# Later column sums and earlier value transposes at the layer boundary of a two-layer hybrid decoder step on one Trainium2 core

## The chip, the cores and the metric

The kernel runs on one core of one Trainium2 chip. The metric is device time in microseconds: before, the median of three runs is 1918.96 us (1916.27, 1918.96 and 1923.78). Lower is better.

## What is computed

One inference step of a decoder with two layers, for 1024 prompt tokens and 8 sample tokens that share the weights. Each layer normalises its input with a root mean square over the 1024 channels, projects it, runs several branches (layer 0: gated delta rule, dilated attention, attention to a memory; layer 1: a gated recurrence and the memory attention), projects back, normalises again and adds the residual. Each layer also projects 256 memory tokens to the keys and values of its memory attention. The part that matters here, from the reference:

```python
def rms_norm(x, g):
    xf = x.astype(F32)
    y = xf * lax.rsqrt(jnp.mean(xf * xf, axis=-1, keepdims=True) + EPS)
    return (y * g.astype(F32)).astype(x.dtype)

def memory_kv(mem, g, w_kv):
    B, M, _ = mem.shape
    return (rms_norm(mem, g) @ w_kv).reshape(B, M, 2, MEM_HEADS, MEM_HD)

    for layer in range(DEPTH):
        mkv_p = memory_kv(mem_prompt, mem_norm[layer], w_mem_kv[layer])
        hp = rms_norm(xp, norm_pre[layer])
        ...
        xp = xp + rms_norm(mix_p.astype(xp.dtype) @ w_out, norm_post[layer])
```

## The kernel before

Channels lie on the 128 partitions (8 tiles of 128 channels), tokens along the free axis. The 1032 tokens are cut into three chunks `CH` of 352, 336 and 344, called 0, 1 and 2. Every large product is made three times in reduced precision (`mm3`, L164 to L166): high part of the weights by high part of the input, high by low, low by high. So each weight tile is loaded, cast to its high part by ScalarE (L152) and subtracted to its low part by GpSimd or VectorE (L154), with three buffers each for the loaded, high and low tiles; the inputs are split in the same way (L228, L229).

The change lies at the boundary of the two layers, in `out_layer` of layer 0. Its second half runs the last output projection over chunk 2 (`one`, products `wo00p2` to `wo07p2`), while chunks 0 and 1 are normalised beside it by generators, `chain(0)` and `chain(1)`; behind it `chain(2)` starts, and `mem_kv(1, ...)` makes the keys (`mk10` to `mk13`) and values (`mv10` to `mv13`) of layer 1 from the 256 memory tokens. Then layer 1 (`odd`) begins with its first products: `wq10` and `wx0` over chunks 0 and 1, then over chunk 2, and `wx1`. The chunk-2 products wait for chunk 2's normalised input `h1..2.`.

A `chain(ci)` makes, for its chunk: the column sums of the post-norm (`po..c`, L199), a reciprocal square root in 12 small VectorE operations on 128x3 elements (L200, L115 to L120) and a diagonal of it (`po..d`, L205); a product with a tile of ones that spreads it over the partitions (`po..b`, L208); the scaling of `y` (L1463) and the residual add (L1464, odd channel tiles on VectorE, even ones on GpSimd). Then the pre-norm of layer 1 in `chan_rstd`: squares on ScalarE (L215), added in pairs on VectorE (L217), column sums `pr.c`, small operations, diagonal `pr.d`, `pr.b`, and `norm_split` (L226 to L229), which writes `h1`.

Each `yield n` in a generator hands control back until the n-th following `tick()`. Every projection ticks once for each chunk it finishes. What a generator issues at a tick is held behind the last instruction that each engine was given at that time; beyond that the scheduler sets the order of each engine's queue. TensorE takes its queue strictly in order: an instruction that waits holds all behind it.

In `mem_kv` each value tile is projected to `vf` with channels on partitions and copied out of PSUM (L323), then turned by two TensorE transposes into a PSUM tile `mvt` (L346) and copied to `vt` by VectorE (L347). For layer 1 this turning is a generator on a lane `turn`; one PSUM buffer (pool `a`, one buffer in this stretch) serves all four.

Of the kernel before, what the change touches and what calls it, by code (L numbers as in the profile page):

```python
# [65 lines left out]
def body(ctx, tc, I, O):  # L66
# [56 lines left out]
    for g in range(3):  # L123
        n = (LEN[g] - 1) * 1024
# [62 lines left out]
            except StopIteration as e:  # L187
                return e.value

    def tok_rstd(pool, sqs, n, scale, name, pt=None):  # L190

        nb = -(-n // P)
        pt = pt or ctile
        cols = pt(f"{name}c")
        x, y, t = (pool.tile([P, nb], F32, name=f"{name}{i}", tag=f"tr{i}{nb}", bufs=2) for i in "xyt")
        for b in range(nb):
            o = min(b * P, n - P)
            for k, sq in enumerate(sqs):
                T.matmul(cols[:, b:b + 1], sq[:, o:o + P], ones[:, 0:1], start=k == 0, stop=k == len(sqs) - 1)  # L199
        V.tensor_scalar(x, cols[:, :nb], scale, EPS, op0=ALU.mult, op1=ALU.add)  # L200
        rsqrt(y, x, t)
        dg = pool.tile([P, CW], F32, name=f"{name}d", tag="dg", bufs=1)
        for b in range(nb):
            o, w = b * P, min(P, n - b * P)
            V.tensor_scalar(dg[:, o:o + w], ident[:, P - w:], y[:, b:b + 1], None, op0=ALU.mult)  # L205
        yield 1
        bc = pt(f"{name}b")
        T.matmul(bc[:, :n], ones, dg[:, :n], start=True, stop=True)  # L208
        return bc[:, :n]

    def chan_rstd(pool, xc, n, name):
        sqs = []
        for k in range(8):
            sq = pool.tile([P, CW], F32, name=f"{name}sq{k}", tag=f"sq{k % 2}", bufs=1 if k % 2 else 4)
            S.activation(sq[:, :n], xc[k], AF.Square)  # L215
            if k % 2:
                V.tensor_tensor(sqs[-1][:, :n], sqs[-1][:, :n], sq[:, :n], ALU.add)  # L217
            else:
                sqs.append(sq)
        yield 1  # L220
        return (yield from tok_rstd(pool, sqs, n, 1.0 / 1024.0, name))

    def norm_split(pool, xc, n, gname, gi, rs, outs, name, hb=2):
        for k in range(8):
# [10 lines left out]
    def start(lane, gen, lag=0):  # L235

        lanes.setdefault(lane, []).append([gen, lag])
# [80 lines left out]
    def mem_kv(l, mem, pool, part=None):  # L318
        outs, rs = mem

        def put(dst, ps):
            if rs is None:
                S.copy(dst, ps)  # L323
            else:
                V.tensor_tensor(dst, ps, rs, ALU.mult)
        if part != 1:
            kts[l] = cst.tile([P, 4, 256], F32, name=f"kt{l}", tag="kt", bufs=1)
            vts[l] = cst.tile([P, 2, 4, P], F32, name=f"vt{l}", tag="vt", bufs=1)
        kt, vt = kts[l], vts[l]
        for h in range(4 if part != 1 else 0):  # L330
            def dk(ci, c0, n, ps, h=h):
                put(kt[:, h, :], ps)
            proj([I["wmem"][l, h]], outs, f"mk{l}{h}", dk, chunks=(0,))
        if part != 1:
            nc.scalar.dma_start(out=O["memk"][l], in_=kt)
        for h in range(4 if part != 0 else 0):
            vf = pool.tile([P, 256], F32, name=f"vf{l}{h}", tag="vf", bufs=2)

            def dv(ci, c0, n, ps, vf=vf):
                put(vf, ps)  # L340
            proj([I["wmem"][l, 4 + h]], outs, f"mv{l}{h}", dv, chunks=(0,))
            nc.scalar.dma_start(out=O["memv"][l, :, h, :], in_=vf)
            def turn(h=h, vf=vf):
                pt = ptile(f"mvt{l}{h}")
                for b in range(2):
                    T.transpose(pt[:, b * P:(b + 1) * P], vf[:, b * P:(b + 1) * P], ident)  # L346
                V.tensor_copy(vt[:, :, h, :], pt[:, :256].rearrange("p (b d) -> p b d", b=2))  # L347
                return
                yield
            if l:  # L350
                start("turn", turn())
            else:
                at_once(turn())

    def silu_drain(pool, dst, dst_s, name):
        def f(ci, c0, n, ps):
# [1028 lines left out]
    def out_layer(l, xa, xa_stack, order, late, w0):  # L1385

        with ExitStack() as so:
# [69 lines left out]
            def chain(ci, xr):  # L1457
                c0, n = CH[ci]
# [5 lines left out]
                    (V if k % 2 else G).tensor_tensor(yk[k], yk[k], xr[k], ALU.add)  # L1464
                if l == 0:
                    nc.scalar.dma_start(out=x1d[:, :, c0:c0 + n], in_=t[:, :, :n])
                    rs = yield from chan_rstd(np_, yk, n, f"pr{ci}")
                    if ci == 2:
                        sx.close()
                        h1.extend(new_h(pool(nst, "h1c", "right"), 1, (2,)))  # L1470
                    norm_split(np_, yk, n, "npre", 1, rs, h1[ci], f"hn{ci}", 2)
                else:
                    for i in range(0, 8, 2):
                        nc.sync.dma_start(out=O["yT"][:, i:i + 2, c0:c0 + n], in_=t[:, i:i + 2, :n])
# [10 lines left out]
            if l == 0:  # L1485
                start("norm2", chain(2, xr[2]))
                tick()
                mem_kv(1, mem_reload(pb), np_)
                drain_lanes("turn")
                drain_lanes("norm2")  # L1490
            else:
                with tc.high_priority(offset=HP):
                    at_once(chain(2, xr[2]))
                sx.close()
# [158 lines left out]
```

## Time and profile before

| | |
|---|---|
| median of three runs | 1918.96 us |
| the profiled execution, whole | 1920.67 us |
| its span in the trace | 1918.9 us |
| TensorE matmuls, busy | 1782.3 us (93%) |
| VectorE, busy | 1088.6 us (57%) |
| ScalarE, busy | 715.0 us (37%) |
| GpSimd, busy | 550.6 us (29%) |
| granted TensorE clock, mean | 0.954 of 2.4 GHz |

Times in the views are microseconds from the span's start. PE is TensorE, DVE is VectorE, ACT is ScalarE, POOL is GpSimd. The trace drops the numbers in tile names (`mk10p0` reads `mk10p`). A row of the timeline gives start, duration, engine, line, operation, output and inputs, shape and count; in brackets stands how long the engine sat idle before it, and what ended that wait.

### The profile page before, as it was taken

What the parts mean: (1) busy time and instruction counts of PE and PEld (TensorE: products, weight loads), DVE (VectorE), ACT (ScalarE), POOL (GpSimd) and SP (SyncE); (2) the same over time, 40 slices, a digit from 0 to 9 for tenths busy, and PEclk for the clock granted to TensorE, in tenths of its full rate; (3) what the DMA queues carried; (4) which work ended last, traced back from release to release, by engine and by line L of the source; (5) the groups of instructions that cost most, each with busy time, mean ns of one, the idle gap of its engine ahead of it and who ended that gap; (6) DMA issues with size and microseconds to landing.
All of it is one profiled execution on the core that took longest, in us unless ns stands there. A gap on an engine that the chain in (4) does not pass through costs nothing.

```text
span 1918.9 us, 29175 instructions
## 1 busy us (share of the span) xinstructions
PE 1782.3 (93%) x11341; PEld 1724.7 (90%) x11341; DVE 1088.6 (57%) x2302; ACT 715.0 (37%) x1610; POOL 550.6 (29%) x367
## 2 busy tenths in 40 slices
PE   7999998798999899999999988998499999989996
PEld 6799998698999899999999977998499999988995
DVE  6878759534543314525336376578735647667536
ACT  5355533122322244333333342344223434526432
POOL 3422224222121113231533403215431534331201
PEclk9999998899999899999999998997699999999998
DMA  8435455543344435545644535465633433223554
GB/s 290 180 132 194 181 165 191 193 135 109 114 179 167 177 137 183 205 149 188 213 168 171 169 118 150 131 202 183 234 108 135 143 133 105 84 67 122 152 186 139
DMA packets 160698, 306.25 MB, mean 160 GB/s; under 512 B 25072, under 2 KB 120496, under 8 KB 158640
## 3 DMA queue, kind: packets, MB, share of 16 engines
q1 hardware_dynamic: 67024, 222.47, 33.7%
q10 hardware_dynamic: 93536, 81.93, 13.2%
q8 instruction: 89, 1.46, 0.3%
q14 instruction: 49, 0.40, 0.1%
HBM read 254.05 MB, written 138.28 MB: 204 GB/s over the span
## 4 chain that ended last, share of the span: by engine, by line
PE 73%; DVE 14%; DMA 3%; ACT 3%; issue 2%; ACTq 1%; SPq 0%; POOL 0%; DVEq 0%; POOLq 0%
PE ss L1016 2%; DVE tm L758 1%; PE so L1049 1%; PE mo L401 1%; PE ms L375 1%; PE gz L881 1%; PE gt L886 1%; PE st L1039 1%; DVE xi L760 1%; DVE y L1463 1%; DMA mg<-mixd 1%; DMA mf<-mixd 1%; PE mt L394 1%; DMA gst<-state_gdn 1%; PE svp L1001 1%
## 5 line engine op out<-in xcount | busy, mean ns | idle before, releaser
L1018 DVE CUSTOM_DVE_ANT_0 spr<-ss,cs 128x128 f32<-128x128 f32 (+1 forms) x96 | 32.4, 350 | 90.7 <-PE ss L1016 90.3
L652 DVE SCALAR_TENSOR_TENSOR acc<-pre,vec,acc 128x1024 f32<-128x1024 f32 x36 | 49.2, 1366 | 13.4 <-ACT acc L650 13.2
L1025 ACT ACTIVATE spr<-spr,snm 128x128 f32<-128x128 f32 (+1 forms) x96 | 42.2, 441 | 36.4 <-DVE snm L1020 36.4
L1464 POOL TENSOR_TENSOR y<-y,xr 128x352 f32<-128x352 f32 (+2 forms) x24 | 23.0, 961 | 106.3 <-DVE y L1463 105.8
L381 ACT ACTIVATE pm<-ms,nm 128x256 f32<-128x256 f32 x64 | 29.7, 473 | 49.1 <-DVE nm L379 42.8
L1424 POOL COPY mg<-mixs 128x8 f32<-128x8 f32 x24 | 9.2, 383 | 131.3 <-DVE wo01al L154 48.6
L1409 DVE TENSOR_TENSOR ya<-ya,ysq 128x352 f32<-128x352 f32 (+2 forms) x42 | 26.2, 625 | 32.7 <-ACT ysq L1408 32.5
L1016 PE MATMUL ss<-sw,sw 128*128 128x128 f32 (+1 forms) x192 | 42.4, 322 | 0.0
L1259 DVE TENSOR_SCALAR lacc<-lpre,vec 128x1024 f32<-128x1024 f32 x8 | 19.3, 2418 | 34.0 <-ACT lpre L1249 34.0
L1049 PE MATMUL so<-spt,svt 128*128 128x128 f32 x280 | 38.2, 275 | 0.0
L401 PE MATMUL mo<-mpt,vt 128*128 128x512 f32 x64 | 34.6, 627 | 3.4 <-DVE mpt L396 3.4
L1049 PEld LDWEIGHTS so<-spt,svt 128*128 128x128 f32 x280 | 36.2, 191 | 0.0
L1427 DVE TENSOR_TENSOR mbl<-mg,mbh 128x344 fp32r<-128x344 f32 x24 | 17.2, 715 | 33.3 <-ACT mbh L1426 33.3
L375 PE MATMUL ms<-kt,qm 128*128 128x256 f32 x128 | 33.4, 390 | 0.0
L1262 DVE SCALAR_TENSOR_TENSOR lacc<-lpre,vec,lacc 128x1024 f32<-128x1024 f32 x24 | 32.7, 1363 | 0.3
L375 PEld LDWEIGHTS ms<-kt,qm 128*128 128x128 f32 x128 | 24.6, 198 | 8.9 <-issue 4.9
L1002 DVE COPY svt<-svp 128x512 f32<-128x512 f32 x24 | 15.5, 685 | 28.9 <-PE svp L1001 24.4
L1016 PEld LDWEIGHTS ss<-sw,sw 128*128 128x128 f32 x192 | 31.2, 189 | 0.6 <-DVE sml L1018 0.2
L758 DVE TENSOR_TENSOR tm<-bl,xi 128x1 f32<-128x1 f32 (+30 forms) x31 | 30.3, 976 | 2.5 <-DMA bl<-aqd 2.0
L1272 POOL TENSOR_TENSOR lxl<-lacc,lxh 128x1032 fp32r<-128x1032 f32 x8 | 22.4, 2800 | 30.6 <-ACT lxh L1271 30.6
L1426 ACT CAST mbh<-mg 128x344 fp32r<-128x344 f32 x24 | 11.5, 481 | 52.4 <-DMA mg<-mixd 42.7
L1308 POOL COPY lhl<-lacc 128x1 f32<-128x1 f32 x8 | 4.5, 559 | 89.7 <-DVE lacc L1307 89.7
(2144 smaller groups left out, 7344.8 us busy)
## 6 DMA issues: line engine op xcount, KB each, us to landing
o_sw3s<-cache_swa SPq DMA_DIRECT2D x64, 1023.5 KB
o_sw2s<-cache_swa SPq DMA_DIRECT2D x16, 1022.0 KB
gaq<-aqd ACTq DMA_DIRECT2D x20, 512.0 KB
mf<-mixd SPq DMA_DIRECT2D x19, 344.0 KB
sfb<-fd SPq DMA_DIRECT2D x12, 512.0 KB
aqd<-aq ACTq DMA_DIRECT2D x4, 1024.0 KB
o_sw3p<-sw SPq DMA_DIRECT2D x8, 512.0 KB
mixd<-lgt ACTq DMA_DIRECT2D x8, 512.0 KB
```

The costliest lines, as they stand in the source:

```text
L375: T.matmul(ps[:, b * 256:(b + 1) * 256], q[:, (b0 + b) * P:(b0 + b + 1) * P], kt[:, h, :], start=True, stop=True)
L381: S.activation(pr[:, b2 * 2 + b, :], ps[:, b * 256:(b + 1) * 256], AF.Exp, bias=nm[:, b0 + b:b0 + b + 1], scale=SC, accum_out=lt[:, b0 + b ...
L401: T.matmul(po, vt[:, kb, h, :], sts[kb], start=kb == 0, stop=kb == 1)
L652: V.scalar_tensor_tensor(acc, pre[:, j:j + 1024], vc("gconv", ti * 4 + j), acc, ALU.mult, ALU.add)
L758: V.tensor_tensor(t3, bl[:, 0:i, i][:, None, :].broadcast_to([P, i, i]), xi[:, 0:i, 0:i].rearrange("p j c -> p c j"), ALU.mult)
L1016: T.matmul(po, q[:, bb * P:(bb + 1) * P], k[:, k0:k0 + w], start=True, stop=True)
L1018: V.tensor_tensor_reduce(pr[:, bb, :w], po, mask, 1.0, NEG, ALU.add, ALU.max, accum_out=ml[:, 0, g, bb:bb + 1])
L1025: S.activation(pr[:, bb, :w], pr[:, bb, :w], AF.Exp, bias=nm[:, bb:bb + 1], scale=SC, accum_out=ml[:, 1, g, bb:bb + 1])
L1049: T.matmul(po[:, (bb % 4) * P:(bb % 4 + 1) * P], vt[:, kb, :], pt[:, o:o + P], start=st, stop=sp_)
L1262: V.scalar_tensor_tensor(acc[:, :1024], pre[:, j:j + 1024], vc("lconv", ti * 4 + j), acc[:, :1024], ALU.mult, ALU.add)
L1409: V.tensor_tensor(acc[:, :n], acc[:, :n], sq[:, :n], ALU.add)
L1464: (V if k % 2 else G).tensor_tensor(yk[k], yk[k], xr[k], ALU.add)
```

## The change

The sums of a chunk's pre-norm are asked for two projections behind its squares instead of one (four for chunk 2), and chunk 2's spread product two behind its sums instead of one. The transposes of layer 1's value tiles are issued directly behind their projection, as layer 0's are, instead of at the next tick.

```diff
-    def tok_rstd(pool, sqs, n, scale, name, pt=None):
+    def tok_rstd(pool, sqs, n, scale, name, pt=None, lag=1):
...
-        yield 1
+        yield lag
         bc = pt(f"{name}b")
...
-    def chan_rstd(pool, xc, n, name):
+    def chan_rstd(pool, xc, n, name, lags=(1, 1)):
...
-        yield 1
-        return (yield from tok_rstd(pool, sqs, n, 1.0 / 1024.0, name))
+        yield lags[0]
+        return (yield from tok_rstd(pool, sqs, n, 1.0 / 1024.0, name, lag=lags[1]))
...
-            if l:
-                start("turn", turn())
-            else:
-                at_once(turn())
+            at_once(turn())
...
-                    rs = yield from chan_rstd(np_, yk, n, f"pr{ci}")
+                    rs = yield from chan_rstd(np_, yk, n, f"pr{ci}", ((2, 1), (2, 1), (4, 2))[ci])
...
                 mem_kv(1, mem_reload(pb), np_)
-                drain_lanes("turn")
                 drain_lanes("norm2")
```

No instruction is added or taken away; the scheduler puts them in another order from `wo05p2` up to the first chunk-2 products of layer 1. Before and behind that each engine's order is the same row for row. Lines behind L346 carry a number lower by three in the changed kernel, and those behind L1486 by four.

TensorE's queue from the end of the value projections on (`mv13`), before: the twelve column sums of chunk 2 (`pr2c`), its spread product, then transposes `mvt11` and `mvt12` in and ahead of layer 1's first product `wq10p0`.

```order
L166 MATMUL mv13p0_13011<-mrh13_12634,mv13l0_13007 128x256
L199 MATMUL pr2c_12743<-cs_72,pr2sq0_12691 128x1
L199 MATMUL pr2c_12743<-cs_72,pr2sq2_12696 128x1
...
L199 MATMUL pr2c_12743<-cs_72,pr2sq6_12706 128x1
L208 MATMUL pr2b_12807<-pr2d_12771,cs_72 128x344
L346 MATMUL mvt11_12999<-cs_72,vf11_12928 128x128 x2
L164 MATMUL wq10p0_13106<-h1h00_11834,wq10h0_13100 128x352
...
L346 MATMUL mvt12_13037<-cs_72,vf12_12966 128x128 x2
L164 MATMUL wq10p0_13106<-h1h06_11846,wq10h0_13100 128x352
```

The same place in the changed kernel; `mvt10` and `mvt11` stand further ahead there, inside `mv12` and `mv13`:

```order
L166 MATMUL mv13p0_13015<-mrh13_12634,mv13l0_13011 128x256
L346 MATMUL mvt12_13004<-cs_72,vf12_12916 128x128 x2
L164 MATMUL wq10p0_13106<-h1h00_11834,wq10h0_13100 128x352
...
L199 MATMUL pr2c_12841<-cs_72,pr2sq0_12691 128x1
L166 MATMUL wq10p1_13132<-h1h15_11860,wq10l0_13101 128x336
...
L199 MATMUL pr2c_12841<-cs_72,pr2sq6_12706 128x1
L165 MATMUL wx0p0_13167<-h1l04_11843,wx0h0_13161 128x352
...
L208 MATMUL pr2b_12949<-pr2d_12869,cs_72 128x344
L164 MATMUL wx0p1_13193<-h1h17_11864,wx0h0_13161 128x336
...
L164 MATMUL wq10p2_13219<-h1h20_12955,wq10h0_13100 128x344
```

The 96 rows of `wq10` and `wx0` over chunks 0 and 1 stood behind `pr2b`; now the sums stand among them, behind the 41st to the 61st, and 93 of them are ahead of `pr2b`.

VectorE's queue at the first turned value tile, before: the copy (L347) stands behind the last split of chunk 2 (`h1l27`), in layer 1's set-up work.

```order
L1246 MEMSET lpre1_13287 128x3
L229 TENSOR_TENSOR h1l27_12828<-hn2hf7_12857,h1h27_12827 128x344
L347 COPY vt1_12639<-mvt10_12961 128x2x128
L1219 TENSOR_SCALAR t8_13069<-e8_13068 128x8
L1227 TENSOR_SCALAR n8_13067<-vec_73 128x8
```

In the changed kernel:

```order
L120 SCALAR_TENSOR_TENSOR po02y_12581<-po02t_12582,po02y_12581 128x3
L347 COPY vt1_12639<-mvt10_12874 128x2x128
L205 TENSOR_SCALAR po02d_12598<-cs_72,po02y_12581 128x128 x2
L205 TENSOR_SCALAR po02d_12598<-cs_72,po02y_12581 128x88
L229 TENSOR_TENSOR h1l13_11857<-hn1hf3_12453,h1h13_11856 128x336
```

The copy of `mvt10` now stands in chunk 2's post-norm, ahead of the diagonal `po02d`; before, it stood behind all of chunk 2's pre-norm.

TensorE's queue at the end of the output projection (`wo07p2`), before: chunk 1's sums stand on both sides of the first key projection, and its spread product `pr1b` in the middle of the third.

```order
L166 MATMUL wo07p2_12538<-mbh07_11825,wo07bl1_12534 128x344
L164 MATMUL mk10p0_12646<-mrh00_12604,mk10h0_12641 128x256
...
L199 MATMUL pr1c_12293<-cs_72,pr1sq0_12186 128x1
...
L166 MATMUL mk10p0_12646<-mrh13_12634,mk10l0_12642 128x256
L199 MATMUL pr1c_12293<-cs_72,pr1sq2_12191 128x1
...
L166 MATMUL mk12p0_12781<-mrh10_12622,mk12l0_12777 128x256
L208 MATMUL pr1b_12378<-pr1d_12321,cs_72 128x336
L199 MATMUL po02c_12579<-cs_72,ya02_11933 128x1 x3
```

In the changed kernel:

```order
L166 MATMUL wo07p2_12538<-mbh07_11825,wo07bl1_12534 128x344
L208 MATMUL pr0b_12312<-pr0d_12255,cs_72 128x352
L199 MATMUL pr1c_12346<-cs_72,pr1sq0_12154 128x1
...
L199 MATMUL pr1c_12346<-cs_72,pr1sq6_12169 128x1
L164 MATMUL mk10p0_12646<-mrh00_12604,mk10h0_12641 128x256
...
L166 MATMUL mv10p0_12815<-mrh12_12630,mv10l0_12811 128x256
L208 MATMUL pr1b_12439<-pr1d_12374,cs_72 128x336
L199 MATMUL po02c_12579<-cs_72,ya02_11933 128x1 x3
L164 MATMUL mv10p0_12815<-mrh13_12634,mv10h0_12810 128x256
```

Chunk 0's spread product `pr0b` stood inside `wo07p2` and now stands directly behind it; all of chunk 1's sums follow it; `pr1b` and the post-norm sums of chunk 2 (`po02c`) have moved behind 54 more rows, into the fifth of the eight projections.

## Rows read from the trace of the kernel before

**Rows 1.** Stretches: length, busy time of PE, PEld, DVE, ACT, POOL; clock; DMA.

```profile
1308.00:1346.00 38.00, 30.36 (x169) 29.79 (x169) 33.20 (x56) 16.42 (x31) 23.87 (x14) 0.69 0.59 192
1346.00:1375.00 29.00, 14.38 (x88) 13.16 (x86) 20.44 (x37) 8.29 (x16) 14.95 (x10) 0.71 0.94 356
1375.00:1386.00 11.00, 0.90 (x4) 0.33 (x3) 8.33 (x21) 3.95 (x9) 3.64 (x4) 0.50 0.05 13
1386.00:1403.00 17.00, 17.00 (x103) 16.97 (x102) 3.40 (x18) 1.72 (x4) 0.00 (x0) 0.92 0.03 9
1403.00:1919.00 516.00, 487.64 (x3009) 472.48 (x3007) 306.42 (x481) 203.67 (x374) 150.81 (x113) 0.98 0.39 128
```

**Rows 2.** TensorE's waits from 1300 to 1403: total, times, longest.

```profile
PE pr2c L199 <- DVE pr2sq L217: 11.5, 4, 7.4
PE mvt L346 <- DVE n L1227: 10.1, 1, 10.1
PE pr1b L208 <- DVE pr1d L205: 3.6, 1, 3.6
PE pr2b L208 <- DVE pr2d L205: 3.1, 1, 3.1
PE mk10p L166 <- POOL mk10l L154: 1.8, 1, 1.8
PE pr1c L199 <- DVE pr1sq L217: 1.7, 1, 1.7
PE mk10p L164 <- ACT mk10h L152: 0.9, 1, 0.9
```

**Rows 3.** Timeline of PE from po02b to the transposes that wait.

```profile
1346.32 0.82 PE L208 MATMUL po02b<-po02d,cs 128*128 128x344 f32 x2
...
1366.97 4.00 PE L199 MATMUL pr2c<-cs,pr2sq 128*128 128x1 f32 x18 [3.23 <-DVE pr2sq L217]
1374.09 1.51 PE L208 MATMUL pr2b<-pr2d,cs 128*128 128x344 f32 x2 [3.12 <-DVE pr2d L205]
1385.71 0.66 PE L346 MATMUL mvt<-cs,vf 128*128 128x128 f32 x2 [10.10 <-DVE n L1227]
```

**Rows 4.** Timeline of DVE: chunk 2's chain, and the copy of the first value tile.

```profile
1349.81 3.95 DVE L1463 SCALAR_TENSOR_TENSOR y<-y,vec,po02b 128x344 f32<-128x344 f32 x8
...
1360.45 0.50 DVE L217 TENSOR_TENSOR pr2sq<-pr2sq,pr2sq 128x344 f32<-128x344 f32 x1
...
1364.50 2.42 DVE L217 TENSOR_TENSOR pr2sq<-pr2sq,pr2sq 128x344 f32<-128x344 f32 x1 [1.40 <-ACT pr2sq L215]
1371.01 0.16 DVE L200 TENSOR_SCALAR pr2x<-pr2c 128x3 f32<-128x3 f32 x1 [4.09 <-PE pr2c L199]
...
1385.15 0.41 DVE L347 COPY vt<-mvt 128x256 f32<-128x256 f32 x1
```

**Rows 5.** Timeline of ACT: the first high parts of chunk 2's input.

```profile
1376.33 0.96 ACT L228 CAST h1h<-hn2hf 128x344 fp32r<-128x344 f32 x2 [11.86 <-DVE hn2hf L226]
```

**Rows 6.** Timeline of PE: column sums and products, two rows in a row each.

```profile
1290.71 2.06 PE L199 MATMUL pr0c<-cs,pr0sq 128*128 128x1 f32 x18
...
1314.64 0.41 PE L164 MATMUL mk10p<-mrh,mk10h 128*128 128x256 f32 x1
1314.86 0.41 PE L165 MATMUL mk10p<-mrl,mk10h 128*128 128x256 f32 x1
...
1402.73 0.32 PE L166 MATMUL wx0p<-h1h,wx0l 128*128 128x336 f32 x1
1402.88 0.31 PE L164 MATMUL wq10p<-h1h,wq10h 128*128 128x344 f32 x1
```

**Rows 7.** Timeline of DVE: chunk 1's small operations.

```profile
1323.28 2.16 DVE L115 TENSOR_SCALAR pr1y<-pr1x 128x3 int32<-128x3 int32 x1
...
1331.30 0.16 DVE L118 TENSOR_TENSOR pr1t<-pr1y 128x3 f32<-128x3 f32 x1
```

**Rows 8.** Timeline of POOL: the subtraction of a weight tile in the same time.

```profile
1322.73 2.68 POOL L154 TENSOR_TENSOR mk12l<-mk12f,mk12h 128x1024 fp32r<-128x1024 f32 x1
```

## The prediction

> **What bounds the kernel now.** I read the stretches first, then TensorE's waits, then the timelines of the engines that it waits for. In the stretches the reader is to see that TensorE is the bound nearly everywhere, and that one place is an exception: behind 1403 it works 487.6 of 516 us at a clock of 0.98, while from 1346 to 1386 it works 15.3 of 40 us, at 0.71 and 0.50 of full speed [rows 1]. That place is the layer boundary, the one that the change reorders. In the list of waits the seven rows add up to 32.7 us of idle TensorE between 1300 and 1403, and two of them make up two thirds: the column sums of chunk 2 wait 11.5 us for their squares, and a value transpose waits 10.1 us for a VectorE copy [rows 2]. Behind both, in TensorE's queue, stand the 96 rows of `wq10` and `wx0` over chunks 0 and 1, which need nothing from chunk 2. In the timelines the reader is to see the chain that makes chunk 2's input: spread product of the post-norm at 1346.3, scaling from 1349.8, square pairs from 1360.5 to 1366.9, sums to 1371.0, small operations, `pr2b` from 1374.1 to 1375.6 [rows 3, 4], and the first high part on ScalarE at about 1376.8, half of the 0.96 us of its two casts behind 1376.3 [rows 5]. Only then comes VectorE's copy of the first value tile, at 1385.2 [rows 4], since it is queued behind chunk 2's split; the second transpose, which needs the same PSUM buffer, goes at 1385.7 [rows 3].
>
> The sum is made against the profiled execution, 1920.7 us; its span is 1918.9, so 1.8 us lie around it. It is 1.7 us above the median of the three runs, 1919.0. Measurement can tell about 0.5% from no change, 9.6 us here.
>
> **What the change does, part by part.** It adds no instruction and no byte, so the sum is of waits alone. I set two marks: the spread product `po02b`, at 1346.3 [rows 3], and the first chunk-2 row of `wq10`, at 1402.9 [rows 6]. Behind the second mark the order is that of before, so what is gained there is kept if the rest is bound by TensorE.
>
> 1. Second stretch, 56.6 us before. The chain of chunk 2 (VectorE, ScalarE, GpSimd) is not shortened: from `po02b` to the first cast it took 1376.8 less 1346.3, 30.5 us. What changes is what TensorE does beside it. Of the 96 free rows 93 now stand ahead of `pr2b`; at full clock one takes 0.15 us (the step between the two products of [rows 6] at 1402.7 and 1402.9), together 14 us, and they go through while squares and small operations run. At half clock they would take about twice that, 28 us, which also fits into 30.5. So the second mark follows `po02b` by 30.5 us rather than 56.6: 26.1 us less. Of the waits, the 10.1 at the transpose goes because the copy of `mvt10` is now issued in chunk 2's post-norm; 11.5 and 3.1 become covered or partly covered; and the 17.0 us of free rows from 1386 to 1403 [rows 1] are no longer spent behind the chain.
>
> 2. Inside that chain a little comes off. The 18 sums that ran at half clock took 4.0 us, the same 18 of chunk 0 at full clock 2.06 [rows 3, 6]. A TensorE with rows to do between the sums should be at the higher clock more of the time; I take half of the 1.9, 1 us. Bounds: 0, and 2.7 if `pr2b`'s 1.5 us halve too. So this stretch gives 27 us.
>
> 3. First stretch, up to `po02b`. Chunk 1's sums move from around the first key projection to ahead of it, and their 1.7 us wait and the 1.8 and 0.9 for the first weights [rows 2] may go. Against that, `pr0b` now stands directly behind the last output product. It waits for a diagonal that VectorE makes behind the last square of that product: a PSUM copy, a square, an add and the diagonal, some 2 us by the nearest row of each kind (a square pair's add takes 0.50 [rows 4], a cast half of 0.96 [rows 5]), with nothing in front of it to cover that. In addition VectorE must finish chunk 0's split before chunk 1's small operations, and that split is interleaved on GpSimd with weight subtractions of some 2.7 us [rows 8]: I put chunk 1's diagonal 2 to 3 us later than before. `pr1b` and chunk 2's post-norm sums also stand 54 product rows further down. Those rows are work that must be done anyway and would stand behind `po02b` otherwise, and TensorE waited 3.6 us at `pr1b` [rows 2], so part of them is covered. Bounds for when `po02b` comes: 8.0 us earlier (1.7, 1.8, 0.9 and 3.6 all gone), and 11.5 later (54 rows at 0.21 us, the half-clock step [rows 6], all on the path). I take 1 us later, since the new 2 us wait and the later diagonal stand about even with the waits that go.
>
> 4. Chunk 0's sums move behind `wo05p2`. They are the same sums on the same engine with its queue full on both sides: 0. Cover gone would show as a wait at `wo06p2` for its low weights, which VectorE now subtracts behind chunk 1's scaling; the scaling of a chunk takes 3.95 us [rows 4], and ahead of that use TensorE has 24 sum passes and twelve product rows, 2.7 and 1.9 us; what is uncovered is below 1 us.
>
> 5. Queues that are passed. SP's load of the first key weights is now issued behind four residual loads and the last output weights; ScalarE's cast of it stands behind two casts of chunk 0 that wait for `pr0b` anyway, so a landing 4 us later costs nothing. GpSimd's subtractions keep their number.
>
> Sum: 1920.7 - 27 + 1 = 1894.7 against the profiled execution, or 1893 on the scale of the median. What is late next, once this goes: the chain of chunk 2 itself, about 30 us, with 16 us of TensorE's work beside it, so some idle time stays.
>
> **The rivals.**
>
> *The first stretch gives back more.* The 54 rows lie wholly on the path to chunk 2's post-norm sums, at half clock, because TensorE again starts and stops there (its clock was 0.69 from 1308 to 1346 [rows 1]). `po02b` is 11.5 us later: 1920.7 - 27 + 11.5 = 1905, or 1904 by the median. For it: VectorE's chain of small operations starts no earlier than before. Against it: before, TensorE waited at exactly this spread product, so some rows are free. Chance 0.20.
>
> *All waits of the first stretch go too.* `po02b` 8 us earlier, with 29 us from the second stretch: about 1884, by the median 1882. For it: the sums stand apart from their squares in both places. Against it: `pr0b`'s new wait. Chance 0.10.
>
> *The time is given back behind 1403.* If layer 1 were paced by transfers or by VectorE, arriving earlier would only lengthen the waits. TensorE's idle time there is 28 of 516 us and the DMA engines are 0.39 busy [rows 1], which speaks against it. 1919. Chance 0.05.
>
> *Slower: VectorE's small operations go one per GpSimd subtraction.* In the trace an operation on three elements took 2.16 us from 1323.28, to within 0.03 us of the end of the GpSimd subtraction that ran then, and its like took 0.16 us at 1331.3 [rows 7, 8]. The change puts subtractions of key and value weights side by side with chunk 1's 12 small operations and 3 diagonal pieces, and more of them with chunk 2's 15. If each of the 30 waited as the one at 1323.28 did, 2.16 us, that is 65 us. Chunk 1's took at least 8 us before (from 1323.3 to 1331.3 it was not yet through), and with as much for chunk 2's it is 49 us more, less the gain of 26: 23 us slower, 1942. It decides from 26 us on, that is from 12 operations caught beyond those caught now. Against it: of GpSimd's subtractions only four stand between chunk 0's split and `h1l10`, which needs `pr1b`, so GpSimd runs dry and the chain gets through. Chance 0.04. The Trainium skill, page "SBUF — State Buffer", section "SBUF: two separate sides", states that GpSimd and a VectorE operation that needs the second port take the shared pair as an exclusive lock for a whole instruction; by that rule every such operation that meets a subtraction waits out the rest of it, which the row at 1323.28 agrees with, and by it alone the price is again bounded by how many subtractions are there to meet.
>
> That the change does not do what it says is excluded by the two orders of TensorE's queue; only for chunk 0 is it nearly so, the sums move by a few rows.
>
> **How the numbers follow.** Forecast 0.61, then 0.20, 0.10, 0.05 and 0.04. Predicted is the forecast's time, 1893. The low end, 1881, takes in the rival with all waits gone; the high end, 1908, the one that gives 11.5 us back, and some more for a chain of chunk 2 that is itself lengthened by subtractions of `wx` weights that it meets. Outside lie no change, slower, and some of each edge. Faster by over 0.5% means below 1909.4: 0.90, the first three cases with a little taken off for their edges. Within 0.5%: 0.06. Slower: 0.04.
>
> **What would show it.** Right: no wait of 10 us at a transpose; TensorE's waits for `pr2sq` under 5 us; the first chunk-2 row of `wq10` some 30 us behind `po02b` and near 1377; a new wait of about 2 us at `pr0b`; `po02b` within 1338 to 1358; the stretch behind the second mark as long as before, 516 us. Wrong: `po02b` far behind 1358 (the first stretch costs more than bounded), `pr2b` more than 35 us behind it (the chain is longer with TensorE's products beside it), or the last 516 us longer by as much as the boundary is shorter.

## The result and the profile after

The changed kernel takes 1896.04 us (median of six runs, 1887.80 to 1899.57); the kernel before, run beside it, 1921.37 us (1909.17 to 1932.74). The ratio is 0.9862, with a 95% interval of 0.9833 to 0.9890. The profiled execution took 1893.15 us, its span 1891.4; forecast were 1894.7 on that scale and 1893 by the median.

Since the orders of both kernels agree up to `wo05p2`, I count from `po00b`, the spread product of chunk 0's post-norm, which lies ahead of everything that moved. The next view gives, for the kernel before, the stretches from `po00b` to the last output product, to `po02b`, to the first chunk-2 row of `wq10`, and to the end. Its columns are those of [rows 1].

```profile
1272.60:1307.40 34.80, 34.80 (x216) 33.93 (x216) 30.85 (x77) 19.05 (x39) 7.47 (x8) 0.95 0.64 207
1307.40:1346.30 38.90, 31.00 (x173) 30.04 (x172) 34.10 (x59) 16.92 (x31) 24.17 (x15) 0.69 0.60 197
1346.30:1402.90 56.60, 31.89 (x188) 30.15 (x188) 31.88 (x74) 13.96 (x29) 18.29 (x13) 0.73 0.49 185
1402.90:1918.90 516.00, 487.74 (x3009) 472.58 (x3008) 306.42 (x481) 203.67 (x374) 150.81 (x113) 0.98 0.39 128
```

The same four stretches of the changed kernel:

```profile
1270.00:1304.40 34.40, 34.27 (x214) 33.44 (x213) 30.96 (x77) 20.34 (x41) 7.47 (x8) 0.95 0.65 217
1304.40:1346.70 42.30, 34.52 (x225) 32.65 (x224) 30.15 (x58) 17.48 (x31) 27.83 (x15) 0.80 0.73 265
1346.70:1375.90 29.20, 23.68 (x140) 22.55 (x138) 18.66 (x43) 10.18 (x22) 10.56 (x9) 0.88 0.67 224
1375.90:1891.40 515.50, 486.85 (x3008) 471.81 (x3008) 319.67 (x513) 206.36 (x381) 155.97 (x117) 0.98 0.39 128
```

The stretch behind `po02b` is 27.4 us shorter, the one ahead of it 3.4 longer, the other two together 0.9 shorter: 24.9 us in all. In the two middle stretches TensorE's idle time fell from 32.6 us (95.5 less 31.00 and 31.89) to 13.3, and its busy time from 62.9 to 58.2 us with the same products and one spread product more, its clock being granted at 0.80 and 0.88 instead of 0.69 and 0.73. So 19.3 us are waits and 4.7 us busy time, which I put down to the clock.

TensorE's waits from 1280 to 1403 in the changed kernel (total, times, longest); they answer to [rows 2]:

```profile
PE pr1b L208 <- DVE pr1d L205: 3.8, 1, 3.8
PE mvt L346 <- DVE vt L347: 3.2, 2, 2.9
PE pr0b L208 <- DVE pr0d L205: 2.1, 1, 2.1
PE mvt L346 <- ACT vf L323: 1.7, 1, 1.7
PE mk11p L164 <- ACT mk11h L152: 0.9, 1, 0.9
PE wq10p L164 <- ACT h1h L228: 0.9, 1, 0.9
PE mk10p L164 <- ACT mk10h L152: 0.7, 1, 0.7
```

The waits for `pr2sq`, for `pr2d` and the one of 10.1 us at a transpose are gone. New are 2.1 us at `pr0b`, 3.2 us at transposes that wait for the copy out of their one PSUM buffer, 1.7 us at one that waits for its value tile, and 0.9 us at the first chunk-2 row. The timeline of PE, as in [rows 3]:

```profile
1346.67 0.74 PE L208 MATMUL po02b<-po02d,cs 128*128 128x344 f32 x2
...
1358.14 0.66 PE L346 MATMUL mvt<-cs,vf 128*128 128x128 f32 x2 [2.90 <-DVE vt L347]
...
1359.16 0.48 PE L165 MATMUL wq10p<-h1l,wq10h 128*128 128x336 f32 x1
1359.44 0.48 PE L166 MATMUL wq10p<-h1h,wq10l 128*128 128x336 f32 x1
...
1366.73 2.06 PE L199 MATMUL pr2c<-cs,pr2sq 128*128 128x1 f32 x18
...
1373.75 0.74 PE L208 MATMUL pr2b<-pr2d,cs 128*128 128x344 f32 x2
...
1375.86 0.42 PE L164 MATMUL wq10p<-h1h,wq10h 128*128 128x344 f32 x1 [0.91 <-ACT h1h L228]
1376.12 0.32 PE L164 MATMUL wx0p<-h1h,wx0h 128*128 128x344 f32 x1
1376.28 0.33 PE L164 MATMUL wx1p<-h1h,wx1h 128*128 128x352 f32 x1
...
1379.84 0.32 PE L165 MATMUL wq10p<-h1l,wq10h 128*128 128x344 f32 x1
```

From `po02b` to the first chunk-2 row it is 29.2 us. The rows of `wq10` and `wx0` over chunks 0 and 1 fill them, in part at half clock: behind the wait of 2.90 us they step by 0.28 us (the granted clock is 0.50 from 1358.1 to 1363.8), and 0.16 from 1363.8 on. The 18 sums (two passes for each of the last nine of chunk 2's twelve) take 2.06 us where they took 4.00.

Behind the first chunk-2 row the order is not that of before. There 24 rows of `wq10` over chunk 2 came in a row. Here one of `wq10` and one of `wx0` are followed by 22 rows of `wx1` over chunk 0, up to 1379.84, and further chunk-2 rows come in groups with rows of `wx1` between them. Chunk 2's split isn't done yet: ScalarE's last cast of it ends at 1383.6, 7.8 us behind the first chunk-2 row. TensorE has no idle time of over 0.15 us from 1376 to 1405, so these rows of `wx1` fill the time that the rest of the split takes.

On VectorE, chunk 2's chain (compare [rows 4]):

```profile
1345.39 0.42 DVE L347 COPY vt<-mvt 128x256 f32<-128x256 f32 x1
...
1351.45 3.94 DVE L1460 SCALAR_TENSOR_TENSOR y<-y,vec,po02b 128x344 f32<-128x344 f32 x8
...
1368.83 0.16 DVE L200 TENSOR_SCALAR pr2x<-pr2c 128x3 f32<-128x3 f32 x1 [5.10 <-PE pr2c L199]
...
1371.20 0.66 DVE L205 TENSOR_SCALAR pr2d<-cs,pr2y 128x128 f32<-128x128 f32 x3
1374.61 1.06 DVE L226 SCALAR_TENSOR_TENSOR hn2hf<-y,vec,pr2b 128x344 f32<-128x344 f32 x2 [2.75 <-PE pr2b L208]
```

The first value tile is copied ahead of `po02b` and no longer behind chunk 2's split. The diagonal is ready at 1371.9, and `pr2b` starts at 1373.75: TensorE is late by 1.9 us now, because the free rows stand in front of it.

### The profile page after: what moved, and what is told of

The parts are those of the page before. It is cut to its first block, busy times and chain, and to the rows that moved or that the text cites. A ratio compares the mean times of both kernels' runs of the same rounds, so it can differ in the third digit from the quotient of the medians.

```text
span 1891.4 us, 29177 instructions
## 1 busy us (share of the span) xinstructions
PE 1773.4 (94%) x11341; PEld 1716.0 (91%) x11341; DVE 1086.6 (57%) x2302; ACT 715.3 (38%) x1610; POOL 550.5 (29%) x367
## 4 chain that ended last, share of the span: by engine, by line
PE 73%; DVE 15%; DMA 5%; issue 3%; ACT 3%; ACTq 1%; POOL 0%; SPq 0%; DVEq 0%; POOLq 0%
PE ss L1013 2%; DVE tm L755 1%; PE so L1046 1%; PE mo L398 1%; PE ms L372 1%; PE gz L878 1%; PE gt L883 1%; PE st L1036 1%; DVE xi L757 1%; DVE y L1460 1%; DMA mg<-mixd 1%; PE mt L391 1%; PE lg L164 0%; DMA mk11f<-wmem 0%; PE lg L166 0%
## 5 line engine op out<-in xcount | busy, mean ns | idle before, releaser
L649 DVE SCALAR_TENSOR_TENSOR acc<-pre,vec,acc 128x1024 f32<-128x1024 f32 x36 | 49.2, 1367 | 13.4 <-ACT acc L647 13.2
L378 ACT ACTIVATE pm<-ms,nm 128x256 f32<-128x256 f32 x64 | 29.7, 473 | 49.3 <-DVE nm L376 42.5
L398 PE MATMUL mo<-mpt,vt 128*128 128x512 f32 x64 | 34.9, 632 | 3.4 <-DVE mpt L393 3.4
L1423 ACT CAST mbh<-mg 128x344 fp32r<-128x344 f32 x24 | 11.5, 481 | 52.5 <-DMA mg<-mixd 42.7
L374 DVE TENSOR_REDUCE nm<-ms 128x2 f32<-128x512 f32 x32 | 21.7, 684 | 15.7 <-PE ms L372 15.7
```

The source lines that it names most:

```text
L378: S.activation(pr[:, b2 * 2 + b, :], ps[:, b * 256:(b + 1) * 256], AF.Exp, bias=nm[:, b0 + b:b0 + b + 1], scale=SC, accum_out=lt[:, b0 + b ...
L398: T.matmul(po, vt[:, kb, h, :], sts[kb], start=kb == 0, stop=kb == 1)
L649: V.scalar_tensor_tensor(acc, pre[:, j:j + 1024], vc("gconv", ti * 4 + j), acc, ALU.mult, ALU.add)
```

## The experiments

The table gives for each kernel the ratio to the kernel before with its interval, and from its profiled execution the time from `po00b` to `po02b`, from there to the first chunk-2 row of `wq10`, from there to the end, and the sum, all in us. Experiments 1 to 4 ran on one chip, each beside the kernel before, and so did 5 to 8 and 9 to 12. The sums are of one execution each.

| kernel | ratio (95%) | to `po02b` | to chunk 2 | to the end | sum |
|---|---|---|---|---|---|
| before | 1 | 73.7 | 56.6 | 516.0 | 646.3 |
| changed | 0.9862 (0.9833 to 0.9890) | 76.7 | 29.2 | 515.5 | 621.4 |
| 1 transposes alone | 0.9908 (0.9879 to 0.9936) | 76.6 | 34.9 | 516.9 | 628.3 |
| 2 lags alone | 0.9934 (0.9909 to 0.9959) | 76.6 | 42.5 | 515.6 | 634.7 |
| 3 changed, again | 0.9874 (0.9850 to 0.9899) | 77.3 | 29.4 | 515.5 | 622.1 |
| 4 key and value lows on VectorE | 0.9858 (0.9830 to 0.9886) | 74.3 | 30.7 | 515.2 | 620.2 |
| 5 chunk 1 one step behind | 0.9920 (0.9895 to 0.9944) | 60.6 | 55.0 | 518.0 | 633.6 |
| 6 as 4, chunk 0's product later | 0.9851 (0.9817 to 0.9884) | 65.9 | 37.4 | 516.2 | 619.4 |
| 7 as 4, first query too | 0.9839 (0.9813 to 0.9864) | 77.3 | 23.4 | 516.1 | 616.8 |
| 8 edits of 6 and 7 | 0.9858 (0.9832 to 0.9885) | 64.1 | 36.6 | 516.1 | 616.8 |
| 9 changed, third time | 0.9858 (0.9824 to 0.9891) | 75.9 | 28.1 | 516.2 | 620.1 |
| 10 as 7, again | 0.9824 (0.9797 to 0.9850) | 74.3 | 23.4 | 516.7 | 614.3 |
| 11 as 7, two transpose buffers | 0.9812 (0.9783 to 0.9841) | 72.6 | 26.2 | 517.6 | 616.4 |
| 12 as 8, two transpose buffers | 0.9830 (0.9797 to 0.9863) | 67.8 | 36.0 | 520.4 | 624.1 |

**1. The transposes alone.** The kernel before, with only this:

```diff
-            if l:
-                start("turn", turn())
-            else:
-                at_once(turn())
+            at_once(turn())
...
-                drain_lanes("turn")
```

> The kernel before with only the transposes moved: each head's value transposes stand directly behind its projection; all column sums keep one step behind their squares. In TensorE's queue the last transposes now stand ahead of the free rows of wq10 and wx0 (chunks 0 and 1), and these rows therefore come between the column sums of chunk 2. My theory (what counts is that the 96 free rows get ahead of the end of chunk 2's chain): the wait of 10.1 us at a transpose goes, the first column sum of chunk 2 still waits about 7 us for its squares (they come some 14 us behind po02b and only part of the rows stand ahead of it), the free rows run inside the chain, and the first chunk-2 row of wq10 comes about 33 us behind po02b where it came 56.6 behind: about 23 us faster, ratio about 0.988. Rival (the transposes give back no more than their own wait): 10 us faster, ratio 0.995, and the first chunk-2 row 46 us behind po02b.

17.3 us faster by the medians (1905.06 beside 1922.38), 18.0 by the sums of the table. Its largest waits on TensorE:

```profile
PE pr2c L199 <- DVE pr2sq L217: 6.1, 1, 6.1
PE pr1b L208 <- DVE pr1d L205: 3.9, 1, 3.9
PE po02b L208 <- DVE po02d L205: 2.3, 1, 2.3
```

The wait of 10.1 us is gone, the one for the squares is 6.1 us (7 expected), and the second stretch is 34.9 us (33 expected): more than the transposes' own wait came off, because the free rows got ahead of the chain's end. It fell 5 us short of my 23, mostly in the first stretch, which I had taken as unchanged and which is 2.8 us longer. Its order is that of before; but on the way to the diagonal of chunk 2's post-norm VectorE meets three subtractions on GpSimd (`mv11` to `mv13`) where it met two, and the diagonal ends 2.8 us later behind `po00b`. What such a meeting costs is the matter of experiment 4.

**2. The lags alone.** The changed kernel with the lines of 1 as they were.

> The changed kernel without the move of the transposes: column sums two or four steps behind their squares, value transposes and their copies where they stood before. In TensorE's queue the sums of chunk 2 and pr2b still stand ahead of the 96 free rows. My theory: the wait at the first sum of chunk 2 (about 11 us) and the one at pr2b (about 3) stay, the free rows are run behind the chain, and only the 10.1 us wait at a transpose becomes shorter, because VectorE's copy of the first value tile stands ahead of chunk 2's split; first chunk-2 row of wq10 about 46 us behind po02b; about 10 us faster, ratio about 0.995. Rival (the lags carry most of the gain, the transposes little): 16 to 26 us faster, ratio 0.987 to 0.992, with no wait over 5 us at the sums of chunk 2.

13.2 us faster by the medians, 11.6 by the sums. TensorE's largest waits:

```profile
PE pr2c L199 <- DVE pr2sq L217: 13.6, 4, 11.9
PE pr1b L208 <- DVE pr1d L205: 3.9, 1, 3.9
PE pr2b L208 <- DVE pr2d L205: 3.1, 1, 3.1
PE pr0b L208 <- DVE pr0d L205: 2.8, 1, 2.8
```

The stretches from the last output product to `po02b` and from there to the first chunk-2 row:

```profile
1306.30:1348.50 42.20, 34.24 (x221) 32.39 (x219) 30.35 (x60) 18.06 (x32) 27.87 (x15) 0.80 0.70 260
1348.50:1391.00 42.50, 25.82 (x141) 24.49 (x142) 28.92 (x76) 13.04 (x28) 14.40 (x12) 0.76 0.49 162
```

As the theory said: the waits at chunk 2's sums and at `pr2b` stay, and the free rows are run behind the chain: all 96 stand behind `pr2b`, where in experiment 1 it is 14 of them. The first chunk-2 row comes 42.5 us behind `po02b` (46 expected). The sums' lag by itself doesn't take the stalls out of the boundary.

**3. Both, on the same chip.** No edit.

> The changed kernel again, on the chip of the two halves, so that the three can be compared. Theory and rivals alike: ratio 0.986 within 0.003. If the parts add up, the gains of the two halves sum to it; by my theory they do not: the half with the transposes alone has most of it.

24.8 us by the medians, 24.2 by the sums; the halves have 18.0 and 11.6. Together they would be 29.6, so about 5 us are counted in both: each half takes the same transpose wait away. Beside experiment 2, where that wait is gone and no free row stands ahead of `pr2b`, moving the transposes and with them 93 rows is worth 12.6 us.

The programs say more about the lags than this. The two numbers for chunk 2, (4, 2), move nothing: with (1, 1) in their place every engine's order is the same row for row. So it is with (1, 1) for chunk 0, where the order is that of experiment 1: chunk 1's two steps do nothing without chunk 0's. What the lags move, chunk 0's and chunk 1's first numbers move together.

**4. Whose subtraction holds the small operations.** In the changed kernel, chunk 1's small operations on VectorE:

```profile
1324.72 0.15 DVE L200 TENSOR_SCALAR pr1x<-pr1c 128x3 f32<-128x3 f32 x1
1324.90 2.18 DVE L115 TENSOR_SCALAR pr1y<-pr1x 128x3 int32<-128x3 int32 x1
1327.12 2.33 DVE L116 TENSOR_SCALAR pr1y<-pr1y 128x3 int32<-128x3 int32 x1
1329.48 2.27 DVE L118 TENSOR_TENSOR pr1t<-pr1y 128x3 f32<-128x3 f32 x1
1331.79 0.16 DVE L119 SCALAR_TENSOR_TENSOR pr1t<-pr1t,pr1x 128x3 f32<-128x3 f32 x1
...
1333.36 0.65 DVE L205 TENSOR_SCALAR pr1d<-cs,pr1y 128x128 f32<-128x128 f32 x3
```

and GpSimd's subtractions in the same time:

```profile
1324.37 2.69 POOL L154 TENSOR_TENSOR mv10l<-mv10f,mv10h 128x1024 fp32r<-128x1024 f32 x1
1327.01 2.41 POOL L154 TENSOR_TENSOR mv11l<-mv11f,mv11h 128x1024 fp32r<-128x1024 f32 x1
1329.38 2.35 POOL L154 TENSOR_TENSOR mv12l<-mv12f,mv12h 128x1024 fp32r<-128x1024 f32 x1
```

Three operations end with three subtractions, to 0.03 us. The edit puts layer 1's key and value subtractions on VectorE:

```diff
-    def proj(aps, x, name, drain, chunks=(0, 1, 2), pace=None):
+    def proj(aps, x, name, drain, chunks=(0, 1, 2), pace=None, eng=None):
-        w = load_w(aps, name)
+        w = load_w(aps, name, eng)
...
-            proj([I["wmem"][l, h]], outs, f"mk{l}{h}", dk, chunks=(0,))
+            proj([I["wmem"][l, h]], outs, f"mk{l}{h}", dk, chunks=(0,), eng=V if l else None)
...
-            proj([I["wmem"][l, 4 + h]], outs, f"mv{l}{h}", dv, chunks=(0,))
+            proj([I["wmem"][l, 4 + h]], outs, f"mv{l}{h}", dv, chunks=(0,), eng=V if l else None)
```

> The changed kernel with the eight subtractions that make the low parts of layer 1's key and value weights on VectorE instead of GpSimd (2.4 to 2.7 us each on GpSimd; about 1.3 on VectorE by the 0.96 us that one of 128x768 takes there). Theory (a small VectorE operation that meets a GpSimd subtraction takes as long as the rest of that subtraction): chunk 1's twelve small operations take 0.15 to 0.17 us each, none over 1 us, and from the first of them to the diagonal it is 8.6 us less 6.3, plus the two or three subtractions that now stand between them, some 5 to 6 us. VectorE has 10 us more to do ahead of it, so the time of the kernel stays within 4 us of the changed kernel's, either way. Rival (the 2.2 us operations have another cause, such as late sums from TensorE): three or so of chunk 1's small operations stay at 2 us and more.

The same operations of chunk 1 on VectorE now:

```profile
1319.46 0.15 DVE L200 TENSOR_SCALAR pr1x<-pr1c 128x3 f32<-128x3 f32 x1
1319.65 0.17 DVE L115 TENSOR_SCALAR pr1y<-pr1x 128x3 int32<-128x3 int32 x1
...
1324.73 0.66 DVE L205 TENSOR_SCALAR pr1d<-cs,pr1y 128x128 f32<-128x128 f32 x3
```

All twelve take 0.15 to 0.17 us, and from the first to the diagonal it is 5.3 us instead of 8.6, with two subtractions of its own between them. So the subtractions were the cause. Chunk 2's post-norm, beside two subtractions that GpSimd kept, still has an operation of 2.29 us and a piece of the diagonal of 2.35. The Trainium skill, page "SBUF — State Buffer", section "SBUF: two separate sides", states that a GpSimd operation and a VectorE operation in a two-port mode or with two SBUF inputs take the shared port pair as an exclusive lock for a whole instruction; the traces agree, with 2.2 us against 0.16. The first operation, at 1324.72, reads its input from PSUM and takes 0.15 us beside a running subtraction. For the kernel it is worth little: the wait of 3.8 us at `pr1b` goes, and one of 3.4 us comes at `po02b`. By the sums it has 620.2 us beside the 621.4, 622.1 and 620.1 of three executions of the changed kernel, by the medians of one chip it is 3.3 us faster, and the intervals of the two ratios overlap: a gain isn't shown.

**5. Chunk 1's lag undone.**

```diff
-                    rs = yield from chan_rstd(np_, yk, n, f"pr{ci}", ((2, 1), (2, 1), (4, 2))[ci])
+                    rs = yield from chan_rstd(np_, yk, n, f"pr{ci}", ((2, 1), (1, 1), (4, 2))[ci])
```

> The changed kernel with chunk 1's column sums one step behind their squares again; chunk 0's stay two steps behind, and the transposes stay where the change put them. In TensorE's queue chunk 1's spread product then stands five rows into the first key projection instead of 119 rows further down, and po02b directly behind the second key projection. My theory (what counts is how many rows that need nothing from a chain stand ahead of its spread product): TensorE waits some 10 to 14 us at pr1b and some 10 us at po02b, chunk 2's chain then lies beside the value projections, and the free rows of wq10 cover its split; about 10 us slower than the changed kernel, ratio to before about 0.992. Rival (an earlier po02b is worth more than the waits ahead of it, since chunk 2's chain sets the end): as fast as the changed kernel or faster, ratio 0.987 or below.

The ratio is 0.992, as the theory had it. Its largest waits on TensorE:

```profile
PE pr1b L208 <- DVE pr1d L205: 6.7, 1, 6.7
PE pr2c L199 <- DVE pr2sq L217: 5.9, 1, 5.9
PE mvt L346 <- ACT vf L323: 5.3, 2, 3.4
```

and its two middle stretches:

```profile
1302.60:1328.40 25.80, 15.48 (x80) 13.35 (x80) 20.72 (x51) 9.23 (x17) 12.07 (x8) 0.60 0.49 177
1328.40:1383.40 55.00, 42.50 (x280) 40.65 (x279) 40.08 (x82) 21.05 (x42) 30.25 (x20) 0.88 0.68 238
```

`po02b` comes 16 us earlier behind `po00b` than in the changed kernel, and the kernel is some 11 us slower (by the ratios; 12.2 by the sums): what counts is TensorE's idle time, 22.8 us in these two stretches beside 13.3, not when one link of the chain comes. The edit moves two things: `pr1b` stands five rows into the first key projection, and `pr2b` ahead of all 96 free rows again. Where TensorE waits I had partly wrong: 10 to 14 us were expected at `pr1b` and 6.7 came, 10 us at `po02b` and none came, and 5.9 us came at chunk 2's sums instead.

**6 to 8. Two edits on top of 4.** In 6 chunk 0's lags are `(2, 2)` in place of `(2, 1)`; 7 puts one more subtraction on VectorE; 8 has both.

```diff
-            e = eng or (V if len(w_loads) < 9 and len(w_loads) % 3 == 0 else G)
+            e = eng or (V if name == "wq10" or (len(w_loads) < 9 and len(w_loads) % 3 == 0) else G)
```

> The kernel of the fourth experiment (key and value low parts on VectorE) with chunk 0's spread product one step later as well (two steps for its sums, two for its product): pr0b stands behind chunk 1's sums, pr1b some 70 rows and po02b some 40 rows earlier than in the fourth experiment. Theory: the wait of 2.9 us at pr0b goes, about 4 us come at pr1b, po02b comes up to 5 us earlier behind the last output product and chunk 2's chain with it: 0 to 5 us faster than the fourth experiment, ratio 0.983 to 0.986. Rival (VectorE, with all the subtractions and both splits in front of chunk 2's chain, sets when po02b comes): waits of 5 us and more at pr1b or po02b, ratio 0.987 to 0.990.

The wait at `pr0b` went, and `po02b` came 8.4 us earlier than in 4; but ahead of it stands a wait of 4.2 us for the cast of the first key weights, in place of the 4 us that I had expected at `pr1b`, and the next stretch is 6.7 us longer, with waits of 5.0 us for a transpose buffer and 4.5 us at chunk 2's sums: 0.8 us faster than 4 by the sums, which is within what two executions of one kernel differ.

> The fourth experiment with one more subtraction, that of the first query weights, on VectorE. In the fourth, chunk 2's post-norm diagonal took 2.7 us and one small operation ahead of it 2.3 us, both beside GpSimd subtractions, and TensorE waited 3.4 us at po02b. If those two were caught by subtractions that now run on VectorE, the diagonal takes 0.66 us and the wait at po02b goes below 2 us; the kernel is 0 to 3 us faster than the fourth. If only chunk 1's splits on GpSimd catch them, nothing changes.

The kernel got 3.4 us faster than 4 by the sums, but not as expected: the diagonal took 1.28 us rather than 0.66, and the wait at `po02b` went from 3.4 to 2.4 only. The gain lies behind `po02b`, 23.4 us instead of 30.7: VectorE's first operation on `pr2c` comes 14.7 us behind `po02b` (19.9 in 4, 22.2 in the changed kernel). Most of it is clock: TensorE's busy time there is 21.5 us at a granted 0.93, and in 4, with nearly as many rows, 27.3 us at 0.73.

> The edits of the sixth and the seventh together. If the first query's subtraction is what delays chunk 2's post-norm and chunk 0's earlier product what brings it forward, this is the fastest of the four: ratio 0.981 to 0.985. If VectorE sets when po02b comes, it is no faster than the sixth.

No better than 7: by the sums the same, by the ratio inside its interval. The forecast of 0.981 to 0.985 was missed, if barely.

**9 to 12. A faster version.** The changed kernel and 7 again on one chip, and 7 and 8 with another split of the PSUM buffers:

```diff
-                split_banks(p=4, a=1, c=3)
+                split_banks(p=3, a=2, c=3)
```

> The changed kernel a third time, as the one that the other three of this group are compared with: ratio 0.986 to 0.988.

> The seventh experiment again (key, value and first query low parts on VectorE), beside the changed kernel. From po00b to the end its trace took 616.8 us, the changed kernel's 621.4 and 622.1: if that holds, 4 to 5 us faster than the changed kernel, ratio 0.984. If it was chance, the two agree within 2 us.

> The seventh experiment with two PSUM buffers for the transposes in place of one, and three for the projections in place of four. Transposes no longer wait for VectorE's copy of the one before (2.9 us in the changed kernel, but only behind a late value tile in the seventh): 0 to 2 us faster than the seventh if the fourth projection buffer is not missed. Against it: with three buffers each projection waits for the drain of the third before it, and the order of TensorE shifts: pr2b comes one row into the last free block, some 40 rows later than in the changed kernel; then 3 to 5 us slower than the seventh.

> The eighth experiment with two PSUM buffers for the transposes and three for the projections. Its largest wait but one was a transpose that waited 4.9 us for VectorE's copy of the one before, with 20 rows of the last value projection and then chunk 2's sums behind it. If the single buffer causes that wait it goes, and the time falls by up to 4 us against the eighth; if chunk 2's squares are late anyway (4.9 us at the first sum), the wait only moves to the sums and the time stays within 2 us.

Experiment 10 has 1889.73 us beside the changed kernel's 1896.20, and by the sums 7 and 10 (616.8, 614.3) lie below all three executions of the changed kernel (621.4, 622.1, 620.1), by 5.6 us in the mean. Experiment 11 has the lowest median, 1887.82, with a sum between those of 7 and 10, so the second buffer shows no gain of its own; nor the loss that I gave it as its rival. In 12 the wait for the transpose buffer went, but the stretch behind the boundary is 520.4 us, 2 to 5 longer than in all the others, which neither reading expected. That is the clock, far from the boundary: TensorE is busy for 492.8 us of that stretch, 488.2 in 8, and from 1688.6 to 1788.6, 320 us behind the first chunk-2 row, it was granted 0.93, where in the same 100 us it was 0.98 in 8 and 1.00 in the changed kernel. Why it fell there stays open. So a sum of one execution can hold some 4 us of clock from far behind the boundary. The edits of 7 make the fastest kernel that two runs bear out, some 0.3% faster than the changed one; the intervals of the ratios overlap, so it is the sums that carry this, two executions against three. Its two middle stretches (experiment 10):

```profile
1305.50:1345.60 40.10, 31.30 (x236) 29.83 (x234) 34.25 (x75) 20.75 (x37) 11.57 (x10) 0.91 0.86 311
1345.60:1369.00 23.40, 22.68 (x127) 21.08 (x127) 12.71 (x36) 6.26 (x15) 6.12 (x6) 0.87 0.60 219
```

TensorE is idle for 9.5 us in them (13.3 in the changed kernel) and busy for 54.0 (58.2), the clock in the first being 0.91.

## Why the prediction was right, and where not

The time was right, 1893 us against 1896.0, and so was its mechanism, with the term of the first stretch 1 to 2.5 us too small and two statements about the change wrong.

1. *Second stretch, 26.1 us less.* It went from 56.6 to 29.2 us, where the first two terms together gave 29.5. Experiments 1 and 2 show the reason: with the free rows ahead of the chain's end it is 34.9, with them behind it 42.5. The prediction's "some idle time stays" holds: 5.5 us, at two transposes (1.7 and 2.9) and at the first chunk-2 row (0.9), and not at `pr2b`, where the free rows themselves are 1.9 us late.

2. *Sums at full clock, 1 us.* The 18 sums went from 4.00 to 2.06 us and `pr2b` from 1.51 to 0.74: the upper bound of 2.7 us was reached in these instructions. It did not all arrive, since TensorE came late to `pr2b`: from `po02b` to `pr2b` it was 27.8 us before and is 27.1 now.

3. *First stretch, 1 us later.* From `po00b` to `po02b` it is 76.7, 77.3 and 75.9 us in three executions, and was 73.7: 2.1 to 3.5 us later. The new wait at `pr0b` is there (2.1 us, as forecast). What was set too low is chunk 1's diagonal: 59.9 us behind `po00b` before, 63.4 now, 3.5 later where 2 to 3 were put, since VectorE began chunk 1's small operations 4.2 us later, behind chunk 0's split, although TensorE was done with the sums 8.8 us sooner. The wait at `pr1b` did not shrink (3.6 before, 3.8 to 4.3 in the three). For the kernel before there is one execution, and experiment 1, with the same order up to there, took 76.6 us: how much of the difference is the change's is not shown.

4. *Chunk 0's sums, 0.* In time this holds: from `po00b` to the last output product it is 34.8 and 34.4 us. The wait that was feared at `wo06p2`, "below 1 us", is not there in the changed kernel's execution, and is 1.4 us in experiment 3. But the prediction saw in chunk 0 "a few rows", and excluded "that the change does not do what it says". Its order is what lets chunk 1's lag act at all, and chunk 2's lag, four and two steps, does nothing. The two orders showed what moves, not which number moves it.

5. *Queues.* The waits for key weights are 0.7 and 0.9 us, where they were 0.9 and 1.8 [rows 2].

6. *The order behind the second mark.* It is not "that of before", as the prediction had it: rows of `wx1` stand among the chunk-2 rows while chunk 2's split goes on. The work ahead of the mark is the same in both kernels, so the stretches can be compared; but no term of the prediction has this move, and what the last stretch would be without it, no run shows.

Of the rivals none came. *The first stretch*: `po02b` came 2.1 to 3.5 us later, neither 11.5 later nor 8 earlier. *Given back behind the boundary*: the last stretch is 515.5 us, was 516.0. *Slower by the lock*: the mechanism is real (experiment 4), but chunk 1's chain has three operations of over 2 us where it had three and one of 0.88 before, chunk 2's post-norm has four of 0.9 to 2.4 us where it had three and two pieces of its diagonal, and chunk 2's twelve of the pre-norm take 0.16 to 0.17 each, so nothing like the 12 further ones came that it needed. It was the number of subtractions that meet a chain that decided, as the prediction argued against it. Part of the close agreement is luck: `po00b` came 2.6 us earlier in the changed kernel's profiled execution than in the other, with the same order ahead of it.

## What to carry to other kernels

Where a strictly ordered engine stalls behind a chain on other engines, count the rows that need nothing from that chain and look where they stand: moving 93 of them ahead of its last link was worth 12.6 us here beyond the wait at the transpose (experiments 2 and 3), more than any wait named in the list, and bringing one link forward by 16 us, with fewer rows ahead of the links, cost some 11 us. An edit of several numbers should be taken apart in the order of the queues, number by number, before one argues about each: here two of the four changed ones did nothing. And moving one engine's work off a shared resource need not pay: here it took 3.3 us off chunk 1's chain, and the next link, at `po02b`, waited for 3.4 us instead.

## What was not expected of the hardware

- The same order of instructions up to `po00b` took from 1267.0 us (experiment 9) to 1280.7 (experiment 1) in the profiled executions, 14 us apart (experiments 11 and 12, where the split of the PSUM buffers changes the order ahead of `po00b` too, are left out), while the rest, from `po00b` to the end, agreed within 2.0 us in three executions of the changed kernel. Differences of a few us between kernels were to be seen only in the second part.
- In the changed kernel the granted clock was 0.60 in the mean from 1291.5 to 1295.5, most of it at the lower of its two levels (1.2 and 2.4 GHz), though TensorE was busy throughout: ahead of it stood 24 passes of one column (chunk 0's twelve sums), in 2.73 us. It falls to the lower level behind these sums in 12 of the 14 profiled executions, the kernel before among them. In experiments 3 and 5 the clock stayed at 1.00 in the same stretch, and TensorE had 1.4 us of idle time there. That idle time began 2.6 us behind the sums, when in the changed kernel the clock had already fallen, so it is not what kept the clock up. What makes the difference stays open.
